# Second token lists of a mixture of experts: fp32 matmuls on raw weights in column groups of the array, and a later second scatter

## The chip, the cores and the metric

The kernel runs as one program on one core of a Trainium2 chip. The core has five engines with their own instruction queues: TensorE (PE in the rows; PEld is its loading of stationary operands), VectorE (DVE), ScalarE (ACT), GpSimd (POOL) and SyncE (SP, which here only issues DMAs), and 16 DMA engines. The metric is the device time of one execution in microseconds; less is better. Each number "before" is of the kernel without the change.

## The reference

One encoder layer of 2048 tokens with 1024 features: normalisation, an input projection, differential attention and retention side by side, an output projection, and then a mixture of experts. The change lies in the mixture alone:

```python
g_prob = jax.nn.softmax((xt @ wg + bg).astype(f32), axis=-1)
g_top_p, g_top_i = lax.top_k(g_prob, 1)
...
top_val, top_idx = lax.top_k(e_logits, MOE_TOP_K)          # 2 of the 8 experts of the group
weights = g_top_p * jax.nn.softmax(top_val, axis=-1)
...
h = jax.nn.silu(xblk @ w_gate[e]) * (xblk @ w_up[e])
return h @ w_down[e]
...
y = jnp.zeros((T + 1, D), f32).at[buf_tok].add(yb.astype(f32) * buf_w[:, None])[:T]
```

There are 32 experts; `w_gate` and `w_up` are 1024 x 512, `w_down` is 512 x 1024, all float32. Each token goes to two experts, and the two weighted results are added to its row of the residual. A final normalisation follows.

## The kernel before

The first 1,250 us compute the projections, attention, retention and the routing. The rest is the mixture, and the change touches nothing ahead of it. Experts are ranked by their number of tokens, and `experts` runs 32 jobs, one expert each, n = 0 to 31. A job has a first list of 128 tokens. The 16 experts with the most tokens have a second list too: 64 rows for ranks 0 to 3 (`CAP64`), 32 rows for ranks 4 to 15. A job with a second list is called heavy here, another light. After two fixed light jobs `MIXED` sets the order: light and heavy by turns (the heavy ones are n = 3, 5, ..., 25, the 64-row ones n = 3, 5, 7, 9), then four heavy ones (n = 26 to 29), then two light ones.

For each job the weights come in 12 pieces of 128 x 1024 floats (512 KB), issued on the SP queue (`load`, L1517): eight for gate and up (`gate_up`, four quarters q with one piece of each), four for `down`. The `down` of job n-1 stands behind the `gate_up` of job n. A piece `mr` lies in one of `RAW` = 9 buffers. `fetch` splits it: ACT makes `mh`, the piece rounded to the array's fast float32 format (L1502), DVE makes the remainder `ml` (L1503). `WP` = 8 pairs of `mh` and `ml` exist. The buffer of `mr` is free again when `ml` is made.

For the first list each product is made of three matmuls in the fast format (`mm3`, L62 to L64): high by high, high by low, low by high. The stationary operand is the 128 tokens' part, the moving one 512 columns of weights. For the second list of m rows the stationary operand holds high and low parts side by side (2m columns), and `mm2` (L71, L72, L74) makes two matmuls of 512 columns in place of three; the results of the high and the low part lie in different rows of two accumulators and are added afterwards (ACT copies one, DVE adds the other: L1600 and L1601 in `gate_up`, L1671 and L1672 in `down`). The parts themselves are made by ACT and DVE as well (L1574 and L1575 for `xov`, L54 and L55 for `hv`).

The results go back to the residual `H` in memory by scatters that add, issued on POOL (`put`, L1678): first the first list's (index `ia`), then the second's (`ib`). A list `apart` names earlier DMAs on `H` that a scatter needn't wait for. POOL also issues the gathers of the tokens (`xg`, `xgo`, L1533), and, for the final normalisation from job 11 on, the loads of 128 finished rows of `H` (`fh`, L1856) and their stores (L1881). ACT squares such rows (`fo`, L1865) between its other work. A scheduler puts the instructions in each engine's order at build time; each engine then runs its own strictly in that order.

## Time and profile before

| | |
|---|---|
| runs | 2036.76, 2047.05, 2047.45 us; median 2047.05 us |
| profiled execution | 2043.92 us, of which the span 2042.1 us |
| PE busy in the span | 1943.3 us (95%) |
| DVE busy | 1546.5 us (76%) |
| ACT busy | 1116.2 us (55%) |
| POOL busy | 560.9 us (27%) |
| DMA, mean | 225 GB/s; 365.62 MB read, 91.75 MB written |

The profile lists for every instruction its engine, source line, start and duration. A matmul's duration includes its way through the array, so that matmuls overlap each other in the rows: the time that one takes from the stream is the distance of the starts. A float32 matmul stands as two instructions in the trace (two passes), one in the fast format as one. Line numbers such as L62 are those of the kernel before.

### The profile page before, as it was taken

How to read it: one execution, taken by the hardware profiler on the slowest of the kernel's cores; microseconds unless marked ns; L12 is line 12 of the kernel's file. 1: busy time of each engine (PE TensorE's matmuls, PEld its weight loads, DVE VectorE, ACT ScalarE, POOL GpSimd, SP SyncE). 2: the span in 40 equal slices, each digit the busy share in tenths (PEclk: the TensorE clock that was granted, in tenths of full speed). 3: DMA queues.
4: the chain of work that ended last, by engine and by line, in shares of the span. 5: the costliest groups of instructions: out<-in, count | busy, mean ns of one | idle time of the engine just before them, and what ended most of it. 6: DMA issues, size and time to landing. Idle time of an engine off the chain costs nothing.

```text
span 2042.1 us, 30287 instructions
## 1 busy us (share of the span) xinstructions
PE 1943.3 (95%) x9811; PEld 1542.0 (76%) x9811; DVE 1546.5 (76%) x3560; ACT 1116.2 (55%) x1895; POOL 560.9 (27%) x293
## 2 busy tenths in 40 slices
PE   7999999999999989889999997999999999999994
PEld 5888888887888877778887875777777677777673
DVE  6355547855666568877778768999998899998974
ACT  4344445633554445555454316767777677776763
POOL 0000000000000000001011105887765677766333
PEclk9999999999999989889999997999999999999997
DMA  6656334573676548364453455999999899998994
GB/s 192 192 165 169 126 117 145 181 232 124 193 225 181 160 128 257 125 213 150 147 179 127 140 227 185 346 324 312 328 319 325 303 354 352 346 344 297 338 320 112
DMA packets 259957, 459.45 MB, mean 225 GB/s; under 512 B 29520, under 2 KB 148304, under 8 KB 258768
## 3 DMA queue, kind: packets, MB, share of 16 engines
q1 hardware_dynamic: 242528, 401.34, 58.1%
q0 software_dynamic: 16976, 55.06, 10.2%
q8 instruction: 79, 1.29, 0.3%
q10 hardware_dynamic: 288, 1.05, 0.1%
q14 instruction: 86, 0.70, 0.1%
HBM read 365.62 MB, written 91.75 MB: 224 GB/s over the span
## 4 chain that ended last, share of the span: by engine, by line
PE 76%; DMA 8%; DVE 5%; POOL 4%; issue 3%; SPq 2%; ACT 2%; ACTq 0%; DVEq 0%; POOLq 0%
PE pa L62 7%; PE pa L63 7%; PE pa L64 7%; PE acc L63 7%; PE acc L64 7%; PE acc L62 7%; PE acc L72 4%; PE acc L74 3%; PE pS L360 3%; PE pS L361 3%; PE pF L64 3%; PE pF L62 3%; PE pF L63 3%; PE pT L392 2%; DMA wr<-in_w_in_dram 2%
## 5 line engine op out<-in xcount | busy, mean ns | idle before, releaser
L1503 DVE TENSOR_TENSOR ml<-mr,mh 128x1024 fp32r<-128x1024 f32 x376 | 446.0, 1213 | 26.4 <-ACT mh L1502 23.6
L1502 ACT ACTIVATE mh<-mr 128x1024 fp32r<-128x1024 f32 x376 | 385.1, 1055 | 117.0 <-PE acc L74 63.1
L1533 POOL DMA_INDIRECT xg<-XN,TA x120 | 279.8, 2332 | 66.2 <-issue 31.1
L362 DVE CUSTOM_DVE_ANT_0 p<-pS,dist 128x512 f32<-128x512 f32 (+2 forms) x320 | 189.0, 607 | 105.5 <-PE pS L361 88.2
L369 ACT ACTIVATE p<-p,nm 128x128 f32<-128x128 f32 (+15 forms) x128 | 153.8, 1202 | 101.8 <-DVE nm L368 101.2
L63 PE MATMUL acc<-ml,xhi 128*128 128x512 f32 x512 | 204.7, 400 | 2.4 <-DVE ml L1503 2.4
L64 PE MATMUL acc<-mh,xlo 128*128 128x512 f32 x512 | 204.7, 400 | 1.9 <-DVE xlo L1575 1.9
L62 PE MATMUL acc<-mh,xhi 128*128 128x512 f32 x512 | 203.0, 399 | 0.7 <-ACT mh L1502 0.7
L54 ACT ACTIVATE ah<-pT 128x512 fp32r<-128x512 f32 (+2 forms) x176 | 85.2, 499 | 152.3 <-PE pT L392 96.7
L62 PE MATMUL pa<-whi,xh 128*128 128x512 f32 x384 | 152.5, 400 | 2.3 <-ACT xh L54 2.3
L62 PE MATMUL pa<-xh,whi 128*128 128x512 f32 x384 | 152.9, 398 | 1.4 <-DVE st L58 1.4
L64 PE MATMUL pa<-whi,xl 128*128 128x512 f32 x384 | 153.6, 400 | 0.0
L63 PE MATMUL pa<-wlo,xh 128*128 128x512 f32 x384 | 153.2, 399 | 0.3 <-DVE wlo L162 0.3
L63 PE MATMUL pa<-xl,whi 128*128 128x512 f32 x384 | 152.0, 396 | 0.0
L64 PE MATMUL pa<-xh,wlo 128*128 128x512 f32 x384 | 151.5, 395 | 0.0
L162 DVE TENSOR_TENSOR wlo<-wr,whi 128x1024 fp32r<-128x1024 f32 x72 | 87.9, 1224 | 65.6 <-ACT whi L161 65.3
L360 PE MATMUL pS<-kst,qs 128*128 128x512 f32 (+1 forms) x320 | 125.9, 398 | 12.0 <-DMA qs<-QS 6.9
L867 POOL TENSOR_TENSOR xc<-xT 128x512 bf16<-128x512 f32 x24 | 31.1, 1299 | 381.7 <-ACT xT L864 331.2
L55 DVE TENSOR_TENSOR al<-pT,ah 128x512 fp32r<-128x512 f32 (+2 forms) x176 | 97.6, 565 | 49.8 <-ACT ah L54 49.4
L161 ACT ACTIVATE whi<-wr 128x1024 fp32r<-128x1024 f32 x72 | 76.0, 1059 | 89.3 <-DMA wr<-in_w_in_dram 41.2
L62 PEld LDWEIGHTS acc<-mh,xhi 128*128 128x128 f32 x512 | 96.8, 189 | 33.0 <-ACT mh L1502 1.1
L626 POOL IOTA dist<- 128x1024 f32 (+2 forms) x3 | 4.2, 1411 | 411.8 <-DVE r L40 404.4
(532 smaller groups left out, 4856.3 us busy)
## 6 DMA issues: line engine op xcount, KB each, us to landing
mr<-in_expert_w_gate_dram SPq DMA_DIRECT2D x128, 512.0 KB
mr<-in_expert_w_up_dram SPq DMA_DIRECT2D x128, 512.0 KB
mr<-in_expert_w_down_dram SPq DMA_DIRECT2D x128, 512.0 KB
wr<-in_w_in_dram SPq DMA_DIRECT2D x72, 512.0 KB
vst<-VS SPq DMA_DIRECT2D x72, 256.0 KB
qs<-QS SPq DMA_DIRECT2D x256, 64.0 KB
st<-in_x_dram SPq DMA_DIRECT2D x16, 512.0 KB
VS<-st SPq DMA_DIRECT2D x32, 256.0 KB
```

What stands on the lines that cost most here:

```text
L54: nc.scalar.activation(hi, ps, AF.Copy)
L55: return nc.vector.tensor_sub(lo, ps, hi.bitcast(F32))
L62: nc.tensor.matmul(out, s_hi, m_hi, start=start, stop=False)
L63: nc.tensor.matmul(out, s_hi, m_lo, start=False, stop=False)
L64: nc.tensor.matmul(out, s_lo, m_hi, start=False, stop=stop)
L162: nc.vector.tensor_sub(lo, r, hi.bitcast(F32))
L360: nc.tensor.matmul(x, q[:, m, 0], ks[m][:, a0:a1], start=True, stop=False)
L362: nc.vector.tensor_tensor_reduce(p[:, a0:a1], x, tab[:, c0 + a0:c0 + a1], SLOPES[h], -3.0e38, OP.add, OP.max, accum_out=cm[:, n:n + 1])
L369: nc.scalar.activation(p[:, :nk], p[:, :nk], AF.Exp, bias=nm, accum_out=s0 if m == 0 else s1)
L1502: self.hi_at = nc.scalar.activation(hi, r, AF.Copy)
L1503: self.lo_at = nc.vector.tensor_sub(lo, r, hi.bitcast(F32))
L1533: nc.gpsimd.indirect_dma_start(out=xg[:, g * 256:(g + 1) * 256], out_offset=None, in_=v, in_offset=bass.IndirectOffsetOnAxis(ap=ix[:, g], ...
```

## The change

The second list's operands stay float32: `xov` is the transposed gather itself and `hv` a plain copy, 128 x m columns per chunk instead of 2m. Its products are single float32 matmuls whose moving operand is the raw piece `mr`. They run in column groups of the array: with m = 64 the gate's 512 columns go to columns 0 to 63 and the up's to 64 to 127; with m = 32 there are four groups with 256 columns each. `down` does the same with its 1024 columns. So one accumulator holds what four did, and nothing has to be added afterwards. A quarter's matmuls for the second list stand behind both of its pieces, in `down` behind two pieces. `mr` is now in use until those matmuls are done; three buffers are added (`RAW2`, by turns with the nine) and one pair of `mh` and `ml` is dropped (`WP` = 7). The second scatter is issued in the next job, behind its first quarter, in jobs from n = 29 on at once; the first scatter is no longer among the DMAs it needn't wait for.

```diff
-def mm2(nc, out, s_hl, m_hi, m_lo, start, stop):
...
+def mm_over(nc, acc, m, x, groups, start, stop):
+
+    for g, w in enumerate(groups):
+        c = slice(g * m, (g + 1) * m)
+        nc.tensor.matmul(acc[c, :w.shape[1]], x, w, start=start, stop=stop, tile_position=(0, g * m))
...
-WP = 8
+RAW2 = 3
+WP = 7
...
-            r = self.load(k, e, part, q)
+            self.n = (self.n + 1) % (RAW + RAW2)
+            r = self.load(k, e, part, q, self.raw2 if self.n < RAW2 else None)
...
-                self.turned(X.xo[:, :, 0:m], X.xo[:, :, m:2 * m], X.xg[1], m // 32)
+                self.turn32(X.xo, X.xg[1], m // 32)
...
-                    mm3(nc, ps[part], X.x[0][:, c], X.x[1][:, c], hi[:, s], lo[:, s], a, z)
-                    if over:
-                        mm2(nc, ps[2 + part], X.xo[:, c], hi[:, s], lo[:, s], a, z)
+                    mm3(nc, ps[part], X.x[0][:, c], X.x[1][:, c], hi[:, s], lo[:, s], c == 0, c == KT - 1)
+            for t in range(2 * over):
+                c, n = 2 * q + t, 8 * m
+                mm_over(nc, ps[2], m, X.xo[:, c], [r[:, a:a + n] for r in rs for a in range(t * 512, (t + 1) * 512, n)],
+                        c == 0, c == KT - 1)
...
-            for i in range(2):
-                nc.scalar.activation(s0[:, i], ps[2 + i][m:2 * m], AF.Copy)
-                nc.vector.tensor_add(s0[:, i], s0[:, i], ps[2 + i][0:m])
-            nc.scalar.activation(s0[:, 0], s0[:, 0], AF.Silu)
-            nc.vector.scalar_tensor_tensor(s0[:, 0], s0[:, 0], X.wo, s0[:, 1], op0=OP.mult, op1=OP.mult)
+            for g in range(gs):
+                nc.scalar.activation(X.ho[:, g * n:(g + 1) * n], ps[2][g * m:(g + 1) * m, :n], AF.Silu)
+            for g in range(gs):
+                c = slice(g * n, (g + 1) * n)
+                nc.vector.scalar_tensor_tensor(X.ho[:, c], X.ho[:, c], X.wo, ps[2][64 + g * m:64 + (g + 1) * m, :n],
+                                               op0=OP.mult, op1=OP.mult)
...
-            split_psum(nc, X.hv[:, :, 0:m], X.hv[:, :, m:2 * m], pt[:, :4 * m].rearrange("p (a b) -> p a b", a=4))
+            nc.scalar.activation(X.hv, pt[:, :4 * m].rearrange("p (a b) -> p a b", a=4), AF.Copy)
...
-                if over:
-                    mm2(nc, ps[2 + half], X.hv[:, t], hi[:, s], lo[:, s], t == 0, t == 3)
+            for i in range(t - 1, t + 1) if over and t % 2 else ():
+                mm_over(nc, ps[2], m, X.hv[:, i], [rs[i][:, a:a + n] for a in range(0, D, n)], i == 0, i == 3)
...
-            for half in range(2):
-                s = slice(half * 512, (half + 1) * 512)
-                nc.scalar.activation(y[:m, s], ps[2 + half][m:2 * m], AF.Copy)
-                nc.vector.tensor_add(y[:m, s], y[:m, s], ps[2 + half][0:m])
-            self.put(y[:m], X.idxo, apart + [st])
+            for g in range(128 // m):
+                nc.scalar.activation(y[:m, g * n:(g + 1) * n], ps[2][g * m:(g + 1) * m, :n], AF.Copy)
+            self.second = (y[:m], X.idxo)
+            if last:
+                self.put_second(apart)
+
+    def put_second(self, apart):
+        if self.second is not None:
+            self.put(*self.second, apart)
+            self.second = None
...
                 if q == 0:
+                    m.put_second(f.loads)
                     for j in ([1, 2] if n == 0 else [n + 2]):
...
-                m.down(jobs[n - 1], f.loads)
+                m.down(jobs[n - 1], f.loads, n >= 29)
```

What this does to the order on PE, in the gate and up part of a job with a 32-row second list (`xhi`, `xlo` are the first list's parts, `xov` the second's; each row a matmul with its output's rows and columns). Before:

```order
7548 L63 MATMUL acc<-ml,xhi 128x512
7549 L64 MATMUL acc<-mh,xlo 128x512
7550 L72 MATMUL acc<-ml,xov 32x512
7551 L74 MATMUL acc<-mh,xov 64x512
7552 L62 MATMUL acc<-mh,xhi 128x512
7553 L63 MATMUL acc<-ml,xhi 128x512
7554 L64 MATMUL acc<-mh,xlo 128x512
7555 L72 MATMUL acc<-ml,xov 32x512
7556 L74 MATMUL acc<-mh,xov 64x512
```

And of the change:

```order
7153 L62 MATMUL acc<-mh,xhi 128x512
7154 L63 MATMUL acc<-ml,xhi 128x512
7155 L64 MATMUL acc<-mh,xlo 128x512
7156 L62 MATMUL acc<-mh,xhi 128x512
7157 L63 MATMUL acc<-ml,xhi 128x512
7158 L64 MATMUL acc<-mh,xlo 128x512
7159 L71 MATMUL acc<-mr,xov 32x256 x8
7160 L62 MATMUL acc<-mh,xhi 128x512
```

Two matmuls behind every three have become one run of eight behind twelve. Not every run stays whole: the order of the change has 118 runs of L71 (85 with 32 rows, 33 with 64) where 16 jobs with six whole runs each would have 96. A cut run, later in the program:

```order
7443 L71 MATMUL acc<-mr,xov 32x256 x2
7444 L63 MATMUL acc<-ml,xhi 128x512
7445 L64 MATMUL acc<-mh,xlo 128x512
7446 L62 MATMUL acc<-mh,xhi 128x512
7447 L63 MATMUL acc<-ml,xhi 128x512
7448 L64 MATMUL acc<-mh,xlo 128x512
7449 L71 MATMUL acc<-mr,xov 32x256 x3
```

On the SP queue, in the stretch of the last heavy jobs, with the engines and DMA queues that each load waits for. Before:

```order
1129 L1517 DMA mr<-in_expert_w_up_dram 128x1024 [waits DMAHW7_49,DVE_49]
1130 L1517 ISA
1131 L1517 DMA mr<-in_expert_w_down_dram 128x1024 [waits DMAHW0_49,DVE_49]
```

And of the change:

```order
1129 L1518 DMA mr<-in_expert_w_up_dram 128x1024 [waits DMAHW7_49,DVE_49]
1130 L1518 ISA
1131 L1518 DMA mr<-in_expert_w_down_dram 128x1024 [waits DMAHW0_49,DVE_49,PE_49]
1132 L1518 ISA
1133 L1518 DMA mr<-in_expert_w_down_dram 128x1024 [waits DMAHW1_49,DVE_49,PE_49]
```

A load into a buffer that a heavy job used waits for PE as well as for DVE. On POOL, in the middle of the jobs (`ia` and `ib` are the two scatters, `TA` and `TBw` index the gathers). Before:

```order
61 L1678 DMA H<-y,ia 2240x1024
62 L1533 DMA xg<-XN_74,TA 128x256 x4
63 L1678 DMA H<-y,ib 2240x1024
64 L1881 DMA out_dram<-fh,perm 2048x1024
65 L1856 DMA fh<-H,perm 128x1024
66 L1533 DMA xgo<-XN_74,TBw 128x256
```

And of the change:

```order
65 L1694 DMA H<-y,ia 2240x1024
66 L1898 DMA out_dram<-fh,perm 2048x1024
67 L1694 DMA H<-y,ib 2240x1024
68 L1534 DMA xgo<-XN_74,TBw 128x256
69 L1534 DMA xg<-XN_74,TA 128x256 x4
70 L1873 DMA fh<-H,perm 128x1024
```

Gathers now stand between the second scatter and the load of finished rows, which must wait for that scatter; fewer stand between the two scatters.

## Rows read from the trace of the kernel before

**Rows 1.** From the profile's page: busy share of PE and of the DMA engines in 40 slices of the span (51 us each), in tenths.

```profile
PE   7999999999999989889999997999999999999994
DMA  6656334573676548364453455999999899998994
```

**Rows 2.** Busy time in three stretches of the mixture: the jobs around the 64-row lists (n = 2 to 10), the other alternating jobs (n = 11 to 25), the last ones. Columns: the stretch, its length, busy us of PE, PEld, DVE, ACT and POOL with counts, TensorE's granted clock, the DMA engines' busy share, GB/s.

```profile
1276.40:1484.50 208.10, 206.16 (x925) 157.58 (x924) 204.08 (x273) 151.61 (x182) 162.47 (x58) 1.00 0.97 326
1484.50:1842.10 357.60, 353.20 (x1547) 257.73 (x1546) 321.44 (x383) 254.96 (x317) 245.83 (x106) 1.00 0.98 336
1842.10:2004.30 162.20, 162.20 (x724) 116.42 (x722) 142.88 (x206) 117.60 (x156) 73.71 (x32) 1.00 0.90 299
```

**Rows 3.** The same view for three pieces of 20 us in which PE is not full.

```profile
1300.00:1320.00 20.00, 19.01 (x82) 14.20 (x81) 20.00 (x24) 14.93 (x18) 18.78 (x5) 1.00 1.00 367
1320.00:1340.00 20.00, 19.31 (x88) 14.60 (x87) 20.00 (x28) 15.18 (x20) 18.48 (x6) 1.00 0.94 308
...
1620.00:1640.00 20.00, 15.60 (x57) 10.03 (x56) 17.03 (x23) 17.49 (x23) 12.06 (x4) 0.91 0.74 218
```

**Rows 4.** PE's timeline in the gate and up part of a 32-row job: start us, duration us, line, output and inputs, stationary operand, moving operand, count.

```profile
1549.09 0.40 PE L64 MATMUL acc<-mh,xlo 128*128 128x512 f32 x1
1549.32 0.39 PE L72 MATMUL acc<-ml,xov 128*32 128x512 f32 x1
1549.55 0.40 PE L74 MATMUL acc<-mh,xov 128*64 128x512 f32 x1
1549.79 0.39 PE L62 MATMUL acc<-mh,xhi 128*128 128x512 f32 x1
1550.02 0.39 PE L63 MATMUL acc<-ml,xhi 128*128 128x512 f32 x1
1550.25 0.40 PE L64 MATMUL acc<-mh,xlo 128*128 128x512 f32 x1
```

**Rows 5.** One line's instructions: L72 in the whole execution (durations least/median/most in ns, first and last start, forms with their counts).

```profile
L72 PE MATMUL acc<-ml,xov x256: 388/392/476, 1305.1 to 1956.1; 128*32 128x512 f32 x96, 128*64 128x512 f32 x32
L72 PE MATMUL acc<-ml,hv x128: 388/392/632, 1345.1 to 1988.1; 128*32 128x512 f32 x96, 128*64 128x512 f32 x32
```

**Rows 6.** PE's timeline in the retention, where float32 matmuls run (L527, L528, L500 on the whole array; L532 is two float32 matmuls in column groups 0 to 63 and 64 to 127, four passes). Columns as in rows 4.

```profile
802.58 0.39 PE L527 MATMUL pF<-state,qz 128*128 128x128 f32 x2
...
803.25 0.39 PE L528 MATMUL pF<-vr,A 128*128 128x128 f32 x2
803.56 0.44 PE L532 MATMUL pF<-vr,kd 128*64 128x128 f32 x4
803.93 0.50 PE L360 MATMUL pS<-kst,qs 128*128 128x512 f32 x1
804.27 0.40 PE L361 MATMUL pS<-kst,qs 128*128 128x512 f32 x1
...
804.97 0.59 PE L500 MATMUL pF<-qz,kt 128*128 128x256 f32 x2
805.40 0.27 PE L501 MATMUL pF<-ident,kt 128*128 128x128 f32 x1
```

**Rows 7.** The same four passes of L532 asked for in two narrow windows: those under way between 803.70 and 803.72 us, and those between 803.728 and 803.80 us.

```profile
L532 PE MATMUL pF<-vr,kd x2: 323/323/323, 803.6 to 803.6; 128*64 128x128 f32 x2
...
L532 PE MATMUL pF<-vr,kd x4: 272/298/323, 803.6 to 803.7; 128*64 128x128 f32 x4
```

**Rows 8.** Who waited for whom from 1240 us to the end: us in total, times, longest us. SPq is the queue that issues the loads.

```profile
ACT mh L1502 <- PE acc L74: 63.1, 53, 3.6
ACT fo L1865 <- DMA fh<-H,perm: 28.9, 6, 9.4
ACT mh L1502 <- DMA mr<-in_expert_w_gate_dram: 2.9, 2, 2.7
...
SPq L1517 <- DVE ml L1503: 380.9, 257, 6.5
```

**Rows 9.** Groups of DVE instructions of the second lists with 32 rows, from 1255 us to the end: output and inputs, shape, count, busy us, mean ns of one, idle time before them.

```profile
L1601 DVE TENSOR_TENSOR s<-s,acc 32x512 f32<-32x512 f32 x24 | 16.1, 671 | 11.1 <-ACT s L1600 10.3 <-ACT sg L1593 0.8
L1672 DVE TENSOR_TENSOR y<-y,acc 32x512 f32<-32x512 f32 x24 | 16.0, 667 | 0.6 <-ACT y L1671 0.6
L1603 DVE SCALAR_TENSOR_TENSOR s<-s,wb 32x512 f32<-32x512 f32 x12 | 8.5, 711 | 0.0
L1575 DVE TENSOR_TENSOR xov<-xT,xov 128x256 fp32r<-128x256 f32 x12 | 5.0, 413 | 0.0
L55 DVE TENSOR_TENSOR hv<-pt,hv 128x128 fp32r<-128x128 f32 x12 | 3.3, 277 | 0.0
```

**Rows 10.** POOL's timeline around one pair of scatters: start us, busy us, line, what.

```profile
1591.77 2.48 POOL L1678 DMA_INDIRECT H<-y,ia  x1 [0.30 <-ACT mh L1502]
...
1605.53 1.39 POOL L1678 DMA_INDIRECT H<-y,ib  x1 [0.30 <-issue]
...
1612.56 1.56 POOL L1856 DMA_INDIRECT fh<-H,perm  x1 [4.31 <-DMA H<-y,ib]
```

**Rows 11.** Busy time as in rows 2, in two short stretches in which DMA runs at its fullest: the first weights ahead of the mixture, and the start of the mixture.

```profile
1185.00:1200.00 15.00, 15.00 (x84) 11.51 (x84) 12.22 (x57) 3.21 (x6) 0.00 (x0) 1.00 1.03 412
1265.00:1280.00 15.00, 14.79 (x59) 11.86 (x60) 14.25 (x14) 13.07 (x15) 11.80 (x9) 0.89 1.02 397
```

More of the change, by code (lines that the diff above doesn't have):

```diff
@@ L64, in mm3 @@
     nc.tensor.matmul(out, s_lo, m_hi, start=False, stop=stop)
-def mm2(nc, out, s_hl, m_hi, m_lo, start, stop):
-    n = s_hl.shape[1] // 2
-    if start:
-        nc.tensor.matmul(out[:2 * n], s_hl, m_hi, start=True, stop=False)
-    nc.tensor.matmul(out[:n], s_hl[:, :n], m_lo, start=False, stop=False)
-    if not start:
-        nc.tensor.matmul(out[:2 * n], s_hl, m_hi, start=False, stop=stop)
+def mm_over(nc, acc, m, x, groups, start, stop):
+    for g, w in enumerate(groups):
+        c = slice(g * m, (g + 1) * m)
+        nc.tensor.matmul(acc[c, :w.shape[1]], x, w, start=start, stop=stop, tile_position=(0, g * m))
 SLOPES = [2.0 ** (-2 * (h + 1)) for h in range(4)]
@@ L1479, in __init__ @@
         self.wp = pool("mw", WP, side="right")
+        self.raw2 = pool("mraw2", RAW2, side="right")
+        self.n, self.second = 0, None
         self.xp = pool("mx", 2)
@@ L1503, in fetch @@
             self.lo_at = nc.vector.tensor_sub(lo, r, hi.bitcast(F32))
-        return hi, lo
+        return hi, lo, r
     @staticmethod
@@ L1557, in rows @@
             m = X.no
-            X.xo = self.tile("xov", [128, KT, 2 * m], F32R, bufs=1)
+            X.xo = self.tile("xov", [128, KT, 64], bufs=1)[:, :, :m]
             if X.ixo is not None:
-                self.turned(X.xo[:, :, 0:m], X.xo[:, :, m:2 * m], X.xg[1], m // 32)
+                self.turn32(X.xo, X.xg[1], m // 32)
                 return
@@ L1565, in rows, with turn32 @@
                 nc.tensor.transpose(pt[:, t * m:(t + 1) * m], xc[:m, t], k.ident[:m, :m])
-            split_psum(nc, X.xo[:, :, 0:m], X.xo[:, :, m:2 * m], pt[:, :KT * m].rearrange("p (a b) -> p a b", a=KT))
+            nc.scalar.activation(X.xo, pt[:, :KT * m].rearrange("p (a b) -> p a b", a=KT), AF.Copy)
+    def turn32(self, x, xg, n):
+        self.k.nc.vector.transpose(x.rearrange("p t (g b) -> p g t b", b=32),
+                                   xg[:, :n * 256].rearrange("p (g a t) -> p g t a", g=n, t=KT))
     def turned(self, hi, lo, xg, n):
@@ L1571, in turned @@
         x = self.tile("xT", [128, KT, 128], bufs=1)[:, :, :n * 32]
-        nc.vector.transpose(x.rearrange("p t (g b) -> p g t b", b=32),
-                            xg[:, :n * 256].rearrange("p (g a t) -> p g t a", g=n, t=KT))
+        self.turn32(x, xg, n)
         nc.scalar.activation(hi, x, AF.Copy)
@@ L1579, in gate_up @@
         over = X.idxo is not None
-        ps = [self.acc.tile([128, 512], F32, name="acc") for _ in range(2 + 2 * over)]
+        m = X.no
+        ps = [self.acc.tile([128, 512], F32, name="acc") for _ in range(2 + over)]
         for q in range(4):
+            rs = []
             for part in range(2):
-                hi, lo = self.fetch(X.e, part, q)
+                hi, lo, r = self.fetch(X.e, part, q)
+                rs.append(r)
                 for t in range(2):
@@ L1596, in gate_up @@
         if over:
-            m = X.no
-            s0 = self.tile("s0", [m, 2, 512], bufs=1)
-            for i in range(2):
-                nc.scalar.activation(s0[:, i], ps[2 + i][m:2 * m], AF.Copy)
-                nc.vector.tensor_add(s0[:, i], s0[:, i], ps[2 + i][0:m])
-            nc.scalar.activation(s0[:, 0], s0[:, 0], AF.Silu)
-            nc.vector.scalar_tensor_tensor(s0[:, 0], s0[:, 0], X.wo, s0[:, 1], op0=OP.mult, op1=OP.mult)
-            X.ho = s0[:, 0]
+            n, gs = 8 * m, 64 // m
+            X.ho = self.tile("s0", [64, 512], bufs=1)[:m]
+            for g in range(gs):
[4 more added lines that the diff above has]
+                                               op0=OP.mult, op1=OP.mult)
     def hidden(self, X):
@@ L1616, in hidden @@
             m = X.no
-            X.hv = self.tile("hv", [128, 4, 2 * m], F32R, bufs=1)
+            X.hv = self.tile("hv", [128, 4, 64], bufs=1)[:, :, :m]
             pt = self.pt.tile([128, 512], F32, name="pt")
@@ L1648, in down_last, with down @@
         C.sum, C.h = C.h, g
-    def down(self, X, apart):
+    def down(self, X, apart, last=False):
         k, nc = self.k, self.k.nc
         over = X.idxo is not None
-        ps = [self.acc.tile([128, 512], F32, name="acc") for _ in range(2 + 2 * over)]
+        m = X.no
+        n = 8 * m
+        ps = [self.acc.tile([128, 512], F32, name="acc") for _ in range(2 + over)]
+        rs = []
         for t in range(4):
-            hi, lo = self.fetch(X.e, 2, t)
+            hi, lo, r = self.fetch(X.e, 2, t)
+            rs.append(r)
             c = slice(t * 128, (t + 1) * 128)
@@ L1664, in down @@
             nc.scalar.activation(y[:, half * 512:(half + 1) * 512], ps[half], AF.Copy)
[L1665 removed]
+        self.put(y, X.idx, apart)
         if over:
             y = self.k.bm.tile([128, D], F32, name="y", tag="m4")
[L1668 to L1673 removed]
+            for g in range(128 // m):
[7 more added lines that the diff above has]
+            self.second = None
     def put(self, y, idx, apart=()):
```

3 lines of the change are left out of this document (removed).

## The prediction

> **What bounds the kernel now.** I read the slices first, then the mixture in three stretches, then who waits for whom, then single instructions. In the slices PE is full almost everywhere, and from the mixture on the DMA engines are full too [rows 1]. By stretch the reader should see PE busy 206 of 208 us, 353 of 358 and 162 of 162, with the DMA engines at 0.97, 0.98 and 0.90 and DVE at 204, 321 and 143 us [rows 2]. So three resources are near their limit, and the waits say which comes first: ACT waits 63.1 us in 53 pieces for matmuls of the second lists to give back a pair `mh`, `ml`, and only 2.9 us for a weight to arrive; the queue of loads waits 380.9 us for buffers that `ml` gives back [rows 8]. Loads are thus early and PE is the bound; where PE has holes, a full DVE stood beside it (1300 to 1340), or ACT had waited up to 9.4 us for rows of the final normalisation (around 1620) [rows 3, 8]. What the change saves on PE counts in full, until the DMA engines or the chain of loads stop it.
>
> **PE, what goes.** L72 has 256 + 128 instructions, and for each L72 there is one L71 or L74: 768 matmuls [rows 5]. In the timeline five instructions take 1550.25 - 1549.09 = 1.16 us, 0.232 each, whatever the width of their stationary operand [rows 4]. So 768 x 0.232 = 178 us go: 12 jobs of 32 rows x 48 = 576, 133.6 us; 4 jobs of 64 rows x 48 = 192, 44.5 us.
>
> **PE, what comes.** A float32 matmul is two passes. Six passes of 128 columns lie between 802.58 and 803.25, 0.112 us each; L500 takes 0.43 us for two passes of 256 columns, 0.215 each [rows 6]; 512 columns should then take 0.43. Do the groups run at once? L532 is the only precedent, and it has two groups. Two of its four passes are under way at 803.70, and all four have started by 803.80 [rows 7]; from the first to the next matmul on the whole array pass 803.93 - 803.56 = 0.37 us, while four passes one after the other need 0.45 without any start or end [rows 6]. So two groups run side by side. For four groups there is no row; the bounds are four at once, and none at once. I take four at once, by the nearest row, which shows no loss with two.
>
> A run lasts as long as its fullest group. In whole runs 12 jobs x 12 chunks are 144 rounds of two 256-column passes, and 4 x 12 = 48 rounds of two 512-column passes; counting the cut runs of the order group by group gives 160 and 54. That is 160 x 0.43 = 68.8 us and 54 x 0.86 = 46.4 us.
>
> Entering and leaving a run costs something. Ahead of L532 the last whole-array pass starts 0.11 after 803.25 and would be through at 803.47; the next whole-array matmul starts at 803.93 and lasts 0.50 where its neighbour lasts 0.40, so its stream begins at about 804.03 [rows 6]. Of these 0.56 us the passes, two at a time, need 2 x 0.112 = 0.22: 0.34 us per run are lost. In rows 4 nothing is lost between stationary operands of 128, 32 and 64 columns, so the lower end is zero. I take 0.34, since L532 is float32 in column groups as the new runs are: 118 x 0.34 = 40 us (28.9 for the 85 runs with 32 rows, 11.2 for the 33 with 64).
>
> The page "TensorEngine Tiling (Array Packing)" of the Trainium skill says under Key Properties that changing the tiling mode, not merely the tile, makes the array drain first. L532 agrees (0.34 us a run), the steady 0.232 of rows 4 with three widths does not, unless the fast format never changes the mode. By the rule the sum is the one below; without it PE saves another 40 us.
>
> Sum on PE: 32-row jobs 68.8 + 28.9 - 133.6 = -35.9 us, or 3.0 a job; 64-row jobs 46.4 + 11.2 - 44.5 = +13.1 us, or 3.3 a job. Together -22.8.
>
> The page "TensorE: Matmul & The Clock Gate" of the Trainium skill, Part 3, Measured speedup vs the span model, gives 2.38 times for three column tiles, which is 0.79 of full overlap. As an estimate from that page the 68.8 us would be 87, and most of the gain in the sum below would be gone; no row here has more than two groups.
>
> **DMA, which takes a part of it back.** The bytes stay the same. In the two fullest stretches the share reads 1.03 and 1.02 at 412 and 397 GB/s [rows 11]: that is the limit. In the middle stretch the share is 0.98 over 357.6 us [rows 2]; at 1.03 the same work needs 340.2 us. So of PE's 8 x 3.0 = 24 us there at most 17.4 can show, and at a share of 1.00 only 7. I take the middle, -12. In the last stretch four 32-row jobs save 12 us and DMA would allow 162.2 x (1 - 0.90/1.03) = 20: -12. In the first the four 64-row jobs cost 13.1 us.
>
> **DVE and ACT.** Per 32-row job DVE loses two adds in `gate_up` (2 x 0.671), two in `down` (2 x 0.667), the low parts of `xov` (0.413) and `hv` (0.277); one product of 512 columns (0.711) becomes two of 256 [rows 9], between 0.71 and 1.42 us together, and I take 0.85, since 256 columns cost 0.413 in the nearest row. That is 3.2 us a job, about 51 us in 16 jobs, of 668 busy in the three stretches. None of it is on the path except where DVE was full and PE had holes: 0.99 + 0.69 us [rows 3], so the first stretch costs +11 instead of +13. ACT trades copies of 512 columns for pieces of 256 of the same total and loses a few; it waits for PE anyway [rows 8]. Were that cover gone, the bound is below 1 us a job.
>
> **The loads.** Before, a load is issued when the piece nine before it has been split, and splitting runs up to eight pieces ahead of PE: 17 pieces. In a heavy job a buffer is now free only when PE has read it, with 12 buffers: 12 pieces, about one job. Queued on SP behind a waiting load are all later loads, and ACT, DVE and PE wait for those. One job is 357.6 / 15 = 23.8 us in the middle stretch [rows 2], and a piece needs 128 rows at DMA's full rate (512 KB at 412 GB/s, 1.3 us) and its turn; I count zero, since ACT hardly ever waited for a weight [rows 8]. What it costs if that cover is too thin is the second rival.
>
> **The scatter.** Before, `ib` stands 13.8 us behind `ia`, and the `fh` load behind it made POOL wait 4.31 us [rows 10]. Now `ib` also waits for `ia` to land, with a store or gathers between them, and gathers stand between it and `fh`. `ib` to `fh` took 1612.56 - 1605.53 = 7.0 us: that is the landing time to be covered. Where `ib` stands right behind `ia` (the last two heavy jobs), POOL waits up to 7 us twice; behind it stand only `fh` loads and stores, for which PE doesn't wait. Bounds 0 and 14 us, or a gain of the 4.4 us of PE that are missing around 1620 [rows 3]; I take zero.
>
> **The sum.** -12 - 12 + 11 = -13 us against the profiled execution of 2043.9 us (span 2042.1, 1.8 around it): 2031. The median of the runs is 3.1 us higher, so I say 2034.
>
> **The rivals.**
> First, runs cost nothing to enter, as between the widths of rows 4. PE then saves 62.9 us, and DMA decides: the first stretch +2, the middle -17.4, the last 4 x (11.1 - 5.7) = -21.5, clipped to -20. Sum -35: 2012. For it: rows 4. Against it: rows 6, the only float32 column groups.
>
> Second, slower: the shorter lead of the loads. Twelve pieces of lead are shared by the raw buffers that PE still holds, so ACT and DVE can't run their seven pieces ahead in heavy jobs; every hold-up of ACT then reaches PE. Before, ACT waited 28.9 us for `fh` [rows 8] and PE lost 4.4 of it around 1620 [rows 3]. If all reaches PE, that is +24.5, and beside the -13 the time is 2058; with loads landing late as well 2070. It decides as soon as the time from a buffer's release to the split of its new piece exceeds what is left of a job. For it: DMA at its limit, where loads land late. Against it: 2.9 us of waits for weights.
>
> Third, slower: four streams don't run faster than two. Then the 32-row rounds take 137.6 us, PE in sum +46: 2093. With no overlap at all (rounds 4 x 68.8 + 2 x 46.4 = 368, plus 40, less 178) +230: 2277. For it: no row with four. Against it: no loss with two.
>
> Fourth, nothing comes of it: DMA gives the middle 7 us, the last stretch 6, and the 64-row jobs take 13: 2047.
>
> **How the numbers follow.** Forecast 0.48 (its own range 2023 to 2043), first rival 0.13, second 0.18, third 0.08, fourth 0.13. Half a per cent, 10 us, is about what a measurement of this kernel can tell from no change. Faster by more: the first rival and two thirds of the forecast, 0.45. Within: the rest of the forecast and nearly all of the fourth, 0.29. Slower: 0.26. The range for 8 in 10 is 2008 to 2076: below, the first rival with a little more; above, the second and a part of what lies toward the third.
>
> **What would show it.** Right: L71 passes of four groups starting within some 10 ns of each other and a round of 32 rows at 0.43 us; about 0.34 us lost around a run; the 15 jobs of the middle (357.6 us before [rows 2]) shorter by some 12 us, the nine around the 64-row lists longer by some 11; DMA share 1.00 or more; ACT waiting for weights now. Wrong: rounds of 0.86 us (third rival), runs without loss (first), PE idle behind `ml` with loads waiting for PE (second).

## The result and the profile after

The change takes 2054.6 us (median of 17 runs) against 2043.2 us of the kernel before: a ratio of 1.0052, interval 1.0032 to 1.0072. One of the 17 took 6493.58 us; it is left out of the ratio. The change is slower by half a per cent; the forecast was 2034. The profiled execution of the change took 2064.1 us (span 2062.3), the upper end of its other runs, so the traces differ by 20 us where the medians differ by 11. Of these 20 us, 5.7 lie ahead of the stretches below, between the silu of the first job and that of the second: 14.5 us before, 20.2 here. e1 and e5 below, two executions of the same order of instructions, have 20.4 and 12.3 there, so this part is not the change's.

By stretch between the same silus as in [rows 2] (each job has one such instruction on ACT, behind its gate and up part), with the end behind the last silu added, the changed kernel reads (length, busy time of each engine, PE clock, DMA share, GB/s):

```profile
1281.20:1502.30 221.10, 219.12 (x917) 139.84 (x917) 195.63 (x252) 143.95 (x169) 117.28 (x59) 0.98 0.89 297
1502.30:1857.90 355.60, 338.83 (x1923) 230.48 (x1922) 300.48 (x333) 243.13 (x318) 187.11 (x103) 0.98 0.94 332
1857.90:2011.20 153.30, 148.07 (x913) 100.27 (x912) 125.86 (x174) 105.20 (x143) 48.31 (x28) 0.98 0.91 316
2011.20:2062.30 51.10, 11.76 (x45) 8.93 (x43) 19.40 (x55) 13.27 (x24) 15.18 (x12) 0.63 0.43 116
```

The end of the kernel before, same view:

```profile
2004.30:2042.10 37.80, 9.41 (x34) 6.78 (x32) 12.73 (x34) 6.06 (x11) 11.17 (x8) 0.66 0.37 113
```

The first stretch is 13.0 us longer, the middle 2.0 and the last 8.9 shorter, the end 13.3 longer. The forecast was 11 longer, 12 and 12 shorter, and no change at the end: most of what it missed are 10 us in the middle and 13 at the end. In the middle PE now stands for 17 us where it stood for 4, at a lower DMA share, so the DMA engines at their full rate aren't what holds it on average.

PE's timeline of the change (start, duration, line, operands) has a whole run of 16 passes and a run of a single matmul that the order cut off:

```profile
1520.24 0.40 PE L64 MATMUL acc<-mh,xlo 128*128 128x512 f32 x1
1520.57 1.07 PE L71 MATMUL acc<-mr,xov 128*32 128x256 f32 x16
1521.57 0.50 PE L62 MATMUL acc<-mh,xhi 128*128 128x512 f32 x1
1521.90 0.40 PE L63 MATMUL acc<-ml,xhi 128*128 128x512 f32 x1
...
1885.57 0.40 PE L64 MATMUL acc<-mh,xlo 128*128 128x512 f32 x1
1885.90 0.62 PE L71 MATMUL acc<-mr,xov 128*32 128x256 f32 x2
1886.45 0.50 PE L63 MATMUL acc<-ml,xhi 128*128 128x512 f32 x1
1886.79 0.40 PE L64 MATMUL acc<-mh,xlo 128*128 128x512 f32 x1
```

From the matmul ahead to the one behind, the whole run takes 1.33 us for eight matmuls and the cut one 0.88 for one; runs of four matmuls, one to a group, take 0.89 (median of 9).

The waits of the change (for what, us in total, times, longest):

```profile
PEld acc L71 <- issue: 44.3, 132, 0.7
ACT fo L1882 <- DMA fh<-H,perm: 32.6, 4, 12.0
POOL H L1694 <- DMA H<-y,ia: 31.0, 5, 9.3
POOL fh L1873 <- DMA H<-y,ib: 11.6, 5, 5.2
...
SPq L1518 <- PE acc L71: 292.6, 95, 11.9
SPq L1518 <- DVE ml L1504: 150.0, 107, 11.2
```

Against [rows 8], ACT waits for `fh` about as long as before but in fewer and longer pieces (the longest, 12.0 us, lies at the end of the kernel), POOL waits 31.0 us for a first scatter to land, and SP waits for PE to give raw buffers back; its longest wait for `ml` has grown from 6.5 to 11.2 us.

One such piece of ACT's, seen on POOL, ACT and PE (start, duration, operation, idle time before it and what ended it):

```profile
1730.22 1.39 POOL L1694 DMA_INDIRECT H<-y,ib  x1 [0.30 <-ACT mh L1503]
1738.05 2.86 POOL L1534 DMA_INDIRECT xg<-XN,TA  x1 [6.44 <-DVE xT L1570]
1741.22 9.31 POOL L1534 DMA_INDIRECT xg<-XN,TA  x1 [0.30 <-issue]
1750.84 0.95 POOL L1534 DMA_INDIRECT xg<-XN,TA  x1 [0.30 <-issue]
1752.09 1.50 POOL L1534 DMA_INDIRECT xg<-XN,TA  x1 [0.30 <-issue]
1753.90 0.94 POOL L1873 DMA_INDIRECT fh<-H,perm  x1 [0.30 <-issue]
...
1750.46 1.99 ACT L1503 ACTIVATE mh<-mr 128x1024 fp32r<-128x1024 f32 x2
1762.06 1.06 ACT L1882 ACTIVATE fo<-fh 128x1024 bf16<-128x1024 f32 x1 [9.61 <-DMA fh<-H,perm]
...
1761.80 0.40 PE L63 MATMUL acc<-ml,hhi 128*128 128x512 f32 x1
1769.71 1.12 PE L1620 MATMUL pt<-ident,sg 128*128 128x128 f32 x4 [7.51 <-DVE sg L1602]
1771.05 0.63 PE L62 MATMUL acc<-mh,hhi 128*128 128x512 f32 x1
1771.48 0.63 PE L63 MATMUL acc<-ml,hhi 128*128 128x512 f32 x1
```

The load of `fh` is issued late, ACT stands 9.61 us in the square that needs it, no weights are split, and PE stands 7.5 us. This `fh` did not wait for a scatter (0.30 us of issue ahead of it). The second scatter had gone at 1730.22; between it and `fh` stand four gathers, which the order of the change puts there: POOL waits 6.44 us for DVE at the first, and the next is busy for 9.31. In the same time the load queue stands: its next load goes at 1752.80, after 11.2 us of waiting for an `ml`, and the first line below, of the windows, shows the DMA engines moving nothing. The loads that catch up then run beside `fh`, which takes 8.2 us from its issue to ACT's start. Which of these made the hold, no run separates. Behind it matmuls start 0.43 us apart instead of 0.234, and the second line shows why: the granted clock is 0.50, 1.2 GHz.

```profile
1744.00:1748.00 4.00, 3.32 (x13) 2.44 (x14) 4.00 (x5) 3.93 (x7) 4.00 (x1) 1.00 0.00 0
...
1769.00:1775.00 6.00, 5.29 (x14) 3.90 (x14) 5.93 (x7) 3.03 (x4) 2.33 (x2) 0.50 1.05 358
```

The end, on POOL:

```profile
1997.17 1.69 POOL L1694 DMA_INDIRECT H<-y,ia  x1 [11.44 <-ACT y L1676]
2008.21 1.35 POOL L1694 DMA_INDIRECT H<-y,ib  x1 [9.35 <-DMA H<-y,ia]
2011.95 1.39 POOL L1873 DMA_INDIRECT fh<-H,perm  x1 [2.40 <-DMA H<-y,ib]
2015.90 2.37 POOL L1694 DMA_INDIRECT H<-y,ia  x1 [2.56 <-ACT y L1676]
2023.56 1.33 POOL L1694 DMA_INDIRECT H<-y,ib  x1 [5.29 <-DMA H<-y,ia]
2027.37 0.99 POOL L1873 DMA_INDIRECT fh<-H,perm  x1 [1.19 <-DMA H<-y,ib]
```

Twice the second scatter waits for the first to land, 9.35 and 5.29 us, with all that is left of POOL's work behind it.

An account of PE for this trace and some of the experiments, worked out from the starts of its matmuls, first silu to end of span, in us. Fast matmuls count 0.234 each; the float32 runs include their entry and exit; "holds" are what is left of the steps between starts, idle and slow clock together; the last line is from the last matmul's start on.

| | before | e8 | change | e1 | e5 | e11 | e15 | e10 |
|---|---|---|---|---|---|---|---|---|
| fast matmuls | 707.6 | 708.1 | 527.0 | 527.4 | 527.4 | 527.4 | 527.4 | 572.1 |
| float32 runs | 0 | 0 | 152.4 | 173.2 | 173.2 | 132.8 | 132.5 | 85.5 |
| their number | 0 | 0 | 118 | 153 | 153 | 90 | 90 | 72 |
| transposes | 23.0 | 23.2 | 23.5 | 24.4 | 24.4 | 22.3 | 22.4 | 22.3 |
| holds | 23.4 | 50.9 | 60.5 | 39.6 | 26.7 | 44.2 | 48.9 | 45.6 |
| after PE | 26.1 | 27.4 | 37.6 | 28.8 | 29.1 | 40.8 | 28.4 | 32.2 |

The change saves 707.6 - 527.0 - 152.4 = 28.2 us of PE's work, loses 37.1 in holds and 11.5 behind PE. Holds between the first two silus differ by up to 8 us from one execution to the next, as said above: 5.7 of the 37.1 are of that kind, and 6.0 of the 27.5 by which e8 stands above the kernel before.

### The profile page after: what moved, and what is told of

The parts are those of the page before. It is cut to its first block, busy times and chain, and to the rows that moved or that the text cites. A ratio compares the mean times of both kernels' runs of the same rounds, so it can differ in the third digit from the quotient of the medians.

```text
span 2062.3 us, 31283 instructions
## 1 busy us (share of the span) xinstructions
PE 1929.6 (94%) x10386; PEld 1482.7 (72%) x10387; DVE 1509.0 (73%) x3476; ACT 1090.1 (53%) x1883; POOL 441.1 (21%) x293
## 5 line engine op out<-in xcount | busy, mean ns | idle before, releaser
L1504 DVE TENSOR_TENSOR ml<-mr,mh 128x1024 fp32r<-128x1024 f32 x376 | 443.3, 1217 | 44.2 <-ACT mh L1503 34.6
L1534 POOL DMA_INDIRECT xg<-XN,TA x120 | 223.8, 1865 | 118.2 <-DVE xT L1570 63.8
L63 PE MATMUL acc<-ml,xhi 128*128 128x512 f32 x512 | 210.6, 411 | 8.8 <-DVE ml L1504 8.7
L62 PE MATMUL acc<-mh,xhi 128*128 128x512 f32 x512 | 210.7, 417 | 3.9 <-ACT y L1676 2.8
L357 PE MATMUL pS<-kst,qs 128*128 128x512 f32 (+1 forms) x320 | 126.4, 400 | 11.6 <-DMA qs<-QS 6.8
L62 PEld LDWEIGHTS acc<-mh,xhi 128*128 128x128 f32 x512 | 98.0, 192 | 52.6 <-issue 13.5
L63 PEld LDWEIGHTS acc<-ml,xhi 128*128 128x128 f32 x512 | 98.6, 193 | 48.4 <-DVE ml L1504 21.3
L358 PE MATMUL pS<-kst,qs 128*128 128x512 f32 (+1 forms) x320 | 117.1, 374 | 0.0
```

Source lines behind the costliest of these rows:

```text
L62: nc.tensor.matmul(out, s_hi, m_hi, start=start, stop=False)
L63: nc.tensor.matmul(out, s_hi, m_lo, start=False, stop=False)
L357: nc.tensor.matmul(x, q[:, m, 0], ks[m][:, a0:a1], start=True, stop=False)
L358: nc.tensor.matmul(x, q[:, m, 1], ks[m][:, a0:a1], start=False, stop=True)
L1504: self.lo_at = nc.vector.tensor_sub(lo, r, hi.bitcast(F32))
L1534: nc.gpsimd.indirect_dma_start(out=xg[:, g * 256:(g + 1) * 256], out_offset=None, in_=v, in_offset=bass.IndirectOffsetOnAxis(ap=ix[:, g], ...
```

## The experiments

Theory A/W: the second scatter's wait for the first is what costs, at the end and, by late `fh` loads, in the middle. Theory B: raw buffers held until PE reads them. Theory C: the 64-row lists. Theory R came later: runs that the order cuts.

**e1, e5: the scatters independent again.** The second scatter depends on the scatters of the job before, but not on the first of its own; loads of H wait for both. e5 also puts it at once.

```diff
-        self.put(y, X.idx, apart)
+        st = self.put(y, X.idx, apart)
...
-            self.put(*self.second, apart)
+            y, idx, st, older = self.second
+            s2 = self.put(y, idx, apart + [st] if older else apart)
+            after(self.k, s2, older)
```

> The changed kernel, with the second list's scatter declared independent of the same job's first one again (as in the kernel before); it still waits for the scatters of the job before, and a load of H for both. Theory A (the end grew because the second scatter of the last jobs waits until the first has landed, 9.35 and 5.29 us in the trace of the change, 0.30 us before): the stretch from the last silu to the end of the span falls from 51.1 to 38-42 us, the second scatter of the last two jobs stands less than 1 us behind the first, and the ratio to the kernel before falls from 1.005 to 0.997-1.000. Rival A2 (y of the last jobs is evacuated late, and the wait lies behind that anyway): the stretch stays at 48-54 us and the ratio at 1.004-1.006.

> The changed kernel with the scatter as in the kernel before: the second list's scatter put right behind the first and declared independent of it; matmuls and buffers are the change's. Theory S (the two parts add: the scatter costs about 21 us, as e2 measured with the old matmuls, and the matmuls gain about 10): ratio 0.993-0.997, ACT's waits of fo for fh below 15 us (32.6 with the change, 56.6 in e2). Rival S2 (the scatter costs only the end's 13 us here and the matmul part itself costs 64-row rounds and lead): ratio 0.998-1.002 with the end at 38-42 us. Rival S3 (late scatters of light and heavy jobs alike were worth something with the new matmuls): above 1.003.

Measured: e1 1.0019 (0.9987 to 1.0052), e5 1.0015 (0.9984 to 1.0047). Both have the same instructions in the same order on every engine, so they are two measurements of one program. The end behind the last silu is 39.4 and 38.8 us, ACT's waits for `fh` 5.1 and 5.5 us, and holds fall from 60.5 to 39.6 and 26.7 (13 us between two executions of one program lie in the first jobs). But with the wait gone the order of PE moved as well: 153 runs, 20.8 us more float32 time. So A's end is there and the ratio isn't; S and A both miss their numbers, since each took PE's order as given. The numbers are those of rival S2: the end pays 13 us for the scatter, the matmuls themselves cost the rest. One of its two reasons, the 64-row lists, e7 bears out; the cut runs (e9) it didn't have.

**e2, e8: the scatter's part alone, on the kernel before.** e8 changes one word of the call:

```diff
-            self.put(y[:m], X.idxo, apart + [st])
+            self.put(y[:m], X.idxo, apart)
```

> The kernel before with the change of the scatter alone: the second list's scatter a quarter job later, at once in the last jobs, and no longer declared independent of the first. Theory A: the stretch from the last silu to the end grows from 37.8 to 46-51 us and the ratio is 1.004-1.007. Rival A2 (the end grew through the new matmul path, by late evacuation): the stretch stays at 36-40 us and the ratio at 0.998-1.002.

> The kernel before with one word of the scatter's change: the second list's scatter is no longer declared independent of the first; its place is the old one. e2 (place and wait together) measured 1.0106. Theory W (the wait for the first scatter's landing does it, by holding POOL's queue and the fh loads behind it): ratio 1.006-1.011, ACT's waits of fo for fh 45-60 us, the end 44-50 us. Rival W2 (the later place does it): ratio 0.998-1.002, waits of fo near 28.9 us. Both in part: 1.003-1.006.

Measured: e2 1.0106 (1.0073 to 1.0139), e8 1.0091 (1.0060 to 1.0122). The order of instructions comes out the same in both, as it did in e1 and e5: the place in the program does nothing, the dependency all of it. It does so in two ways that no run separates: by the wait itself, and by the other order into which the scheduler puts the instructions (against the kernel before, the traces of e8 differ in some 30 places on PE, 35 on ACT, 62 on DVE and 17 on POOL). The waits of e8:

```profile
ACT fo L1865 <- DMA fh<-H,perm: 64.0, 9, 10.5
...
POOL H L1678 <- DMA H<-y,ia: 29.7, 5, 7.4
```

And one chain of it, on POOL and PE:

```profile
1989.39 1.62 POOL L1678 DMA_INDIRECT H<-y,ia  x1 [9.34 <-ACT hv L54]
1996.73 4.82 POOL L1678 DMA_INDIRECT H<-y,ib  x1 [5.72 <-DMA H<-y,ia]
...
2007.22 1.50 POOL L1856 DMA_INDIRECT fh<-H,perm  x1 [4.38 <-DMA H<-y,ib]
...
2010.79 0.39 PE L64 MATMUL acc<-mh,xlo 128*128 128x512 f32 x1
2017.23 0.79 PE L62 MATMUL acc<-mh,hhi 128*128 128x512 f32 x1 [6.05 <-ACT hhi L1613]
2017.82 0.63 PE L63 MATMUL acc<-ml,hhi 128*128 128x512 f32 x1
2018.24 0.63 PE L62 MATMUL acc<-mh,hhi 128*128 128x512 f32 x1
```

`ia` to `ib` to `fh`, each behind the landing of the one before; ACT stands 10.5 us; PE stands 6 and then runs at half clock. W holds for the ratio, and its waits are beyond their range (64.0 us); in e2 the ratio is above A's range. Both are refuted at the end, which stays at 36.5 us in e8 and 37.2 in e2. The loss lies ahead of it, in e8 in holds of 50.9 us instead of 23.4. So the longer end of the change needs more than the dependency; that it needs the dependency too, e1, e5 and e15 show.

**e3, e4, e6: the lead of the loads.** e3 lets the float32 matmuls read `mh`; e4 (on the change) and e6 (on e5) have other numbers of buffers.

```diff
-                rs.append(r)
+                rs.append(hi.bitcast(F32))
...
-RAW2 = 3
-WP = 7
+RAW2 = 5
+WP = 6
```

> The changed kernel, whose fp32 matmuls for the second lists read the high part of the weights (mh) in place of the raw buffer; the low part of the weights is left out for those rows. PE, ACT, DVE and the scatters have the same instructions; a raw buffer is free once DVE has made ml. Theory B (raw buffers held until PE has read them shorten the lead of the loads, and that ate the middle's gain): the DMA queue's waits for PE at the load fall from 292.6 us to below 60, PE's idle time over the three stretches falls by 8 us or more, the middle stretch from 355.6 to 342-349 us, and the ratio to 0.998-1.001. Rival B2 (the lead costs nothing; the 64-row jobs and the end explain it all): the waits fall as well, but the middle stretch stays within 3 us of 355.6 and the ratio at 1.003-1.006. A third way: mh, now held up to a quarter longer, is what stops ACT; then ACT's waits of mh for PE grow beyond 81.5 us and the ratio is above 1.006.

> The changed kernel with 9 + 5 raw buffers and 6 pairs of mh and ml, in place of 9 + 3 and 7. Theory B (lead of loads): the DMA queue's waits for PE fall from 292.6 us to 150-230, the middle stretch by 3-8 us, the ratio to 1.000-1.003. Rival B2 (lead costs nothing): ratio 1.004-1.006 and the middle within 2 us. If the pairs bind instead: ACT's waits of mh for PE grow from 81.5 to over 110 us and the ratio is above 1.006.

> The kernel of e5 with 9 + 5 raw buffers and 6 pairs in place of 9 + 3 and 7. Theory B (the lead of the loads costs part of the middle's gain): ratio 0.002-0.005 below that of e5, the middle stretch 3-8 us shorter. Rival B2 (e4's gain over the change was chance of where its scatters fell): within 0.0015 of e5.

Measured: e3 1.0060 (1.0032 to 1.0088). The waits of SP for PE are gone from its queue, and only these are left:

```profile
SPq L1518 <- DVE ml L1504: 408.0, 263, 9.6
```

Yet the middle is 355.0 us: B's cause removed, and no gain. It isn't clean, since ACT now waits 94.6 us for PE to give `mh` back, as the third way said, and PE has a hold of 9.7 us. e4 gave 1.0004 (0.9982 to 1.0027), faster than the change and where B put it, but SP's waits for PE stayed at 293.4 us; it has 105 runs in place of 118, which may be the reason. e6 gave 0.9999 (0.9974 to 1.0023), its wait 270.4 against 279.2 us of e5, and no difference that can be measured. B is not supported, and not excluded for single holds such as that at 1762.

**e7: the old path for 64 rows.** On e5; 9 + 4 raw buffers and 6 pairs. Its core (`down` and the evacuations likewise):

```diff
+                    if m == 64:
+                        mm2(nc, ps[2 + part], X.xo[:, c], hi[:, s], lo[:, s], c == 0, c == KT - 1)
-            for t in range(2 * over):
+            for t in range(2 * (m == 32)):
```

> The kernel of e5 with the old matmul path (two weight parts in the fast format) for the 64-row lists and the new one for the 32-row lists; 9 + 4 raw buffers and 6 pairs, since the old path's buffers take the room of one raw buffer more. Theory C (four jobs with 64 rows cost 13.1 us more on PE by the arithmetic of rounds): the first stretch (silu 2 to silu 11) falls by 10-14 us against e6 and the ratio lies 0.005-0.007 below e6's. Rival C2 (this stretch waits for something else as well, so PE's time there isn't paid in full): it falls by 0-5 us, ratio within 0.002 of e6's.

Measured: 0.9961 (0.9930 to 0.9993), 0.0038 below e6. The first stretch is 208.4 us against 220.1: 11.7 us, as C says, of which the ratio shows two thirds, less than C's 0.005.

**e9, e10, e11: runs kept whole**, on e1, e7 and the change. Each float32 matmul is put behind the last fast one of its quarter, with priority:

```diff
-        nc.tensor.matmul(acc[c, :w.shape[1]], x, w, start=start, stop=stop, tile_position=(0, g * m))
+        with k.tc.high_priority(300), k.tc.issue_after(k.mm.ins):
+            k.nc.tensor.matmul(acc[c, :w.shape[1]], x, w, start=start, stop=stop, tile_position=(0, g * m))
```

> The kernel of e1 (the change, scatters independent) in which every run of float32 matmuls is issued whole: they are put behind the last fast matmul of their quarter, ahead of other PE work. In e1 and e5 the order cuts them into 153 runs (118 in the change, 96 now); from 118 to 153 runs the trace has their float32 time grow from 169 to 195 us while 31 fast gaps of 0.235 drop out of the count, so about 0.53 us per cut. Theory R (cut runs ate the gain of e1 and e5): 57 cuts fewer, up to 30 us of PE; where the DMA engines allow only a part of it in the middle, ratio 0.989-0.996 against 1.0019 of e1. Rival D (the DMA engines at 0.98 in the middle and the splitting of weights bound it, so PE's time is only exchanged for idling): ratio 0.998-1.002.

> The kernel of e7 (new path for 32 rows alone, scatters as before; 0.9961) with whole runs: 72 in place of 117. Theory R: up to 24 us of PE, ratio 0.985-0.992, the fastest kernel of this study. Rival D: 0.994-0.998.

> The change with its own scatter (it waits for the first) and whole runs, 90 in place of 118. Theory R with W (cut runs and the scatter's wait are separate costs): 28 cuts fewer at 0.53 us, 10-15 us off the change's 1.0052: ratio 0.998-1.001, with ACT's waits of fo for fh still over 25 us. Rival (the wait holds the pace, PE's saving vanishes in it): 1.003-1.006.

Measured: e9 0.9952 (0.9925 to 0.9979), e10 0.9868 (0.9829 to 0.9907), e11 0.9934 (0.9908 to 0.9960). R holds in all three, in e11 by more than forecast; ACT's waits for `fh` fell there to 15.7 us, which wasn't. The gain of e11 over the change, 0.0118 or 24 us, is larger than the 19.6 us of float32 time saved; in the traces holds fell too (60.5 to 44.2, 7.8 of it between the first two silus). That e9, without the wait, isn't faster than e11, with it, was not expected: e9's holds are 60.0 us, 7.5 of the difference again between the first two silus, and why is open.

**e12, e14: the square later**, on e8 and the change:

```diff
-                    if q and n < 31:
-                        column(n - 3, q - 1)
+                    if q == 2 and n < 31:
+                        column(n - 3, 0)
...
                 if q == 3 and n < 31:
+                    column(n - 3, 1)
                     column(n - 3, 2)
```

> The kernel of e8 (before, with the wait for the first scatter's landing; 1.0091) in which ACT's square of the rows for the final normalisation is issued a quarter job later, so the load of these rows has about 6 us more to land before ACT stands at it. Theory W (POOL's wait delays the fh load, ACT stands in the square waiting for it with the splitting of weights behind it, and PE runs dry): ACT's waits of fo for fh fall from 64 us to below 30 and the ratio to 0.999-1.005. Rival (POOL's wait costs by another way, such as the gathers of rows behind it): ratio stays at 1.007-1.011.

> The change, with ACT's square of the rows for the final normalisation issued a quarter job later; PE's order is the change's, instruction for instruction. Theory F (the late fh loads hold ACT, ACT holds PE, and PE's clock falls behind each hold): ACT's waits of fo for fh fall from 32.6 us to below 12, the clock stays at 1.00 in the middle stretch (0.98 with the change), ratio 0.998-1.002. Rival F2 (these waits are hidden by the pairs that ACT is ahead): ratio 1.004-1.007. In e12 the same edit took the waits from 64 to 48.6 us and the ratio from 1.0091 to 1.0067, less than expected, so a part of either may show: 1.002-1.004.

Measured: e12 1.0067 (1.0042 to 1.0093), e14 1.0045 (1.0019 to 1.0071). Neither tells anything: on ACT the square stands where it stood. In e12 mainly DVE's part moved; in e14 the traces show the order of the change on every engine, so that it is a second measurement of the change, and PE stands 7.8 us at the same place as in the rows above. That ACT's hold makes PE's is read from the traces, not shown by an experiment.

**e13, e15, e16: the wait taken away in the last two jobs only**, on the change, on e11, and on e11 with the old path for 64 rows (the line against that of e1):

```diff
-            s2 = self.put(y, idx, apart + [st] if older else apart)
+            s2 = self.put(y, idx, apart + [st] if last else apart)
```

> The change, with the second list's scatter declared independent of the first in the last two jobs alone (28 and 29 in order, where it is put at once); PE's order is the change's, instruction for instruction. Theory A (the wait for the first scatter's landing, twice, lengthens the end): the second scatter stands about 0.3 us behind the first there (9.35 and 5.29 before), the stretch from the last silu to the end falls from 51.1 to 38-43 us, the ratio from 1.0052 to 0.998-1.001. Rival A2 (job 29's y is evacuated late by ACT, and the end hangs on that): the stretch falls by less than 4 us, ratio 1.003-1.006.

> The kernel of e11 (the change with whole runs, 0.9934, end of 52.8 us) with the last two scatters of second lists independent as in e13. Theory A: the end falls by about 11 us, ratio 0.986-0.990. Rival A2: 0.992-0.995.

> The kernel of e15 with the old matmul path for 64-row lists (9 + 4 raw buffers, 6 pairs): the change's late scatters, independent in the last two jobs, new path in whole runs for 32 rows alone. Theory C and R together: another 5-10 us off e15, ratio 0.981-0.986, below e10's 0.9868. Rival D (in the middle the DMA engines at 0.98-0.99 bind already, and the late scatters with their wait cost something against e10): 0.986-0.992.

Measured: e13 1.0037 (1.0011 to 1.0064). PE's order is the change's, and on POOL

```profile
1992.02 1.69 POOL L1708 DMA_INDIRECT H<-y,ia  x1 [13.00 <-ACT y L1682]
1994.01 1.35 POOL L1708 DMA_INDIRECT H<-y,ib  x1 [0.30 <-issue]
2003.55 1.01 POOL L1889 DMA_INDIRECT fh<-H,perm  x1 [8.20 <-DMA H<-y,ib]
```

the second scatter stands 0.30 us behind the first, but `fh` waits 8.20 us for it in turn: 2003.55 is 11.5 us behind `ia`, where the change needs 14.8. The end falls by 5.0 us, between theory and rival, and the ratio by less than can be told, into the rival's range. In e15 the same edit takes the end from 52.8 to 39.3 us and the ratio to 0.9856 (0.9823 to 0.9889), 16 us below e11: A in full there. e16 gave 0.9834 (0.9799 to 0.9868), the lowest ratio, within the error of e10 and e15; its profiled execution, the slowest of five, has an end of 49.5 us although the second scatter stands 0.3 us behind the first, and why is open. The stretches of e15:

```profile
1282.10:1496.50 214.40, 210.41 (x915) 138.10 (x916) 195.58 (x252) 143.90 (x169) 130.14 (x59) 0.98 0.90 306
1496.50:1833.00 336.50, 322.57 (x1850) 224.33 (x1849) 298.86 (x332) 242.92 (x315) 183.57 (x102) 0.99 0.97 344
1833.00:1984.00 151.00, 149.55 (x998) 102.61 (x996) 129.90 (x182) 108.50 (x154) 59.63 (x33) 1.00 0.99 343
1984.00:2023.30 39.30, 9.55 (x34) 6.44 (x32) 16.37 (x46) 10.90 (x18) 8.58 (x8) 0.64 0.43 130
```

## Why the prediction was wrong, step by step

- **PE, what goes:** right. The trace has 768 fast matmuls fewer, 179.7 us at 0.234; 178 were forecast. (By the table it is 772, since four more of the change's stand ahead of its first silu.)
- **PE, what comes:** right. 152.4 us against 155.2. The four groups of a round start within 0.02 us of each other, and their passes 0.216 us apart, so that a round takes the forecast 0.43. Entry and exit cost the forecast 0.34 us: from 1520.24 to 1521.57 pass 1.33 us, the next matmul lasts 0.10 longer than its neighbours, 0.23 belong to the matmul ahead and 0.86 to the two rounds; PEld's waits, 44.3 us in 132 pieces, are 0.34 each too. This agrees with the rule that a change of tiling mode drains the array ("TensorEngine Tiling (Array Packing)" of the Trainium skill, Key Properties). The float32 format isn't the reason: in the kernel before, a float32 matmul on the whole array (L500 at 804.97) starts 0.23 us behind a fast one, with no loss. The first and third rivals are out.
- **64 rows dearer by 13:** right, by the first stretch (+13.0) and by e7 (11.7).
- **DMA takes a part back:** wrong as a limit. For the middle it said "at 1.03 the same work needs 340.2 us"; e15 and e10 pass through it in 336.5 and 336.0 us at shares of 0.97 and 0.99 and 344 and 353 GB/s, so the share isn't a scale on which work can be stretched. In the change the share even fell.
- **DVE and ACT:** DVE is busy 46.4 us less over the three stretches; 51 were forecast. The first stretch is 13.0 us longer, not 11, so that the 1.7 us that this was to take off don't show.
- **"The loads ... I count zero":** not refuted by e3 and e6, though SP now waits 292.6 us for PE. The second rival got the sign and, at 2058, nearly the time. It had the path, a hold-up of ACT that reaches PE; its cause, the shorter lead, is not shown, and at the longest hold, where the load queue stood, not excluded.
- **"The scatter ... I take zero", with 0 and 14 us as bounds: the step that failed.** It saw that POOL would wait twice in the last heavy jobs, up to 7 us each, and put this at nothing, since "behind it stand only `fh` loads and stores, for which PE doesn't wait". The waits came, 9.35 and 5.29 us, and the end is 13.3 us longer: the loads of `fh`, their squares and their stores are the last work of the kernel, whether PE waits for them or not. Taking the wait away in the last two jobs gives back 5.0 us of the end in e13, and 13.5 in e15, where the time falls by 16. Nor is it so that PE doesn't wait for `fh`: each engine runs in order, the square of `fh` stands on ACT ahead of splits of weights, and PE needs these. On the kernel before, the dependency costs 0.9 per cent, 18.6 us, with the end unchanged and ACT waiting 64.0 us for `fh` in place of 28.9 (e8). [rows 8] already had the path and [rows 3] what it cost; the second rival used both for the loads, and the step on the scatter didn't.
- **What no step had:** a hold of PE costs more than its length, by the clock behind it (below). The 10 us that are missing in the middle are about what the one hold at 1762 costs, 7.5 us and then 5.6 us of matmuls at half clock; that is read from traces (e13 and e14 have the same hold, 7.7 and 7.8 us), not shown by an experiment. And 118 runs were priced rightly and then taken for granted: with whole runs, and the wait gone in the last two jobs, the same idea is worth 1.4 per cent (e15).

What stays open: how much of the change's own loss in the middle is the wait. Taking it away there changed PE's order too, with whole runs (e9 against e11) it didn't show, and the longest hold has no wait for a scatter right ahead of it.

## What to carry to other kernels

A dependency on an engine that does little but issue DMAs has to be followed to the next in-order engine that waits for what is queued behind it, from there to the bound, and to the end of the kernel. When short matmuls in column groups are added, keep each run of them whole in the order: a run of one matmul costs PE nearly what a round of four does. And before an experiment's ratio is read, compare its order of instructions with the one it is held against; several of these edits moved something else, or nothing.

## What the runs showed that was not expected

Behind the long holds of PE the granted clock was 0.50, 1.2 GHz: the 7.5 us at 1762 were followed by matmuls 0.43 us apart until about 1775, and in e8 the 6 us at 2011 likewise. Not every hold did this: in e1 PE stood 3.2 us at 1807 and the clock stayed at 1.00. The page "TensorE: Matmul & The Clock Gate" of the Trainium skill says, under Loop structure matters more than you think, that a long wait between matmuls lets the clock drop and that those behind it run cold; the two holds first named agree. One gather on POOL was busy for 9.31 us at 1741 where its neighbours took 0.95, with the DMA engines empty from 1743 on. It isn't alone: e13 and e14 have it at the same place in the order (9.32), and the kernel before has one of 14.03 us at 1849.6, with DMA at a share of 0.74. Nothing here says why.
